# First group of attention: two of five pieces of a combination on VectorE, the last Fourier parts on three PSUM banks

## The chip, the cores and the metric

The kernel runs on one core of one Trainium2 chip. The core has five engines with an instruction queue each: TensorE (PE; its weight loads are shown as PEld), VectorE (DVE), ScalarE (ACT), GpSimd (POOL) and SyncE (SP, which issues transfers). On-chip memory is SBUF; the results of TensorE land in PSUM, which has eight banks of 128 partitions by 512 f32 columns. The metric is the device time of one execution in microseconds, as the median of several runs; less is better.

## What is computed

One layer of a diffusion backbone for 256 context ("prompt") tokens and 2048 latent tokens of width 1024: a modulated norm, one projection to queries, keys, values and Fourier channels, differential attention in four heads, a Fourier transform over positions and channels in four groups of 128 channels, an output projection, and a squared-ReLU MLP. What matters here, cut from the reference:

```python
def one_block(qblk):                      # differential attention
    s = jnp.einsum('bqhmd,bkhmd->bhmqk', qblk, k).astype(jnp.float32) * scale
    p = jax.nn.softmax(s, axis=-1)
    a = p[:, :, 0] - lam * p[:, :, 1]
    return jnp.einsum('bhqk,bkhe->bqhe', a.astype(v.dtype), v)
...
def fourier_mix(f, w_four):
    b, n, _, _ = f.shape
    spec = jnp.fft.fft2(f.astype(jnp.float32), axes=(1, 3), norm='ortho').real.astype(f.dtype)
    return jnp.einsum('bngc,gce->bnge', spec, w_four).reshape(b, n, FOUR_WIDTH)
...
def merge(attn, four, subln_g, lam_init, w_out):
    ...
    return jnp.concatenate([a.reshape(b, n, ATTN_WIDTH), four], axis=-1) @ w_out
```

Per query and head there are two score rows (m = 0 and 1), each with its own softmax over 2560 keys; the second, scaled by lambda and the ratio of the two sums, is subtracted from the first, and the difference multiplies the values.

## The kernel before

The kernel runs through stages: norm and projection, the Fourier transform, attention, output projection and MLP. Matrix products that need f32 accuracy are made of three matmuls on split operands (`mm3`, lines 86 to 88: high by high, high by low, low by high), so an operand that comes out of PSUM is split into a rounded high part (a ScalarE cast) and a low part (a VectorE subtraction).

**The Fourier part (lines 645 to 835).** The transform over 2048 positions is folded into shorter ones. For each part and each of the four channel groups g, `ab` makes two products A and B over positions, each in a PSUM tile of the tag "ab" (five banks), and `evac` (lines 669 to 674) splits them: the cast to `abh` at L672, the subtraction into `abl` at L673. Then `yT` (lines 650 to 661) multiplies A and B by the channel matrices of the group into a tile `py` of the tag "y" (three banks), and a ScalarE copy at L661 puts it into the group's output tile `ys`, with a stride that interleaves the frequencies. All parts but the last make two such halves for a group, one for the rising and one for the mirrored frequencies. The loop over the parts (lines 819 to 833) runs "p" (the prompt), "e", "f" and "l", with 256, 256, 128 and 256 columns for A and B each; the product `py` of a group stands one group behind its A and B in program order, so that the split is done meanwhile. When a group's part "l" is copied, ScalarE issues the transfer of `ys` to DRAM (`four`, L698). The last product of part "l" of group 3 is the last TensorE work before attention.

**Attention (lines 838 to 1156).** A `Head` holds keys and values of one head, a `Group` 256 queries of it in two halves j of 128 rows. For a group, `fill(j, m, b)` writes the scores of 512 keys into one PSUM bank (two matmuls, L918), so there are 2 x 2 x 5 = 20 fills per group; `rowmax` (VectorE, L923) takes the maximum of the bank, `comb` (L926) that of the five, negated; `exp` (ScalarE, L942) writes the exponentials into `P0s` for m = 0 or `P1s` for m = 1 with their sum and thereby frees the bank. `combine(j)` (lines 944 to 966) makes the factor (L946 to L948) and adds the scaled `P1s` into `P0s`: on GpSimd in two parts of 1024 and 1536 columns, each a scaling (L964) and an addition (L965), or, as far as `vcomb` says, on VectorE in pieces of 512 columns with one instruction each (L954). Before, `vcomb` is 5 for the first group (first head, g = 0) and for the last one, and 0 for all others; it applies to j = 1 only. Then come transpositions (`tr`, L974), splitting (`ah`, L980; `al`, L985) and the product with the values (`mul`, L998).

Attention's PSUM is one pool: five banks of the tag "S", two of the tag "pt" for the transpositions and one, "po", for the output. Fills use "S". For the first and second group and for the last one, `bank` counts fills (`edge`) and lets two of seven consecutive fills use "pt" as well, because no transpositions run then.

The order of the work on every engine is that of the program text here: the events of all groups are put into a list with planned times (a step takes T, five exps), sorted, and written out under `manual_schedule`. Every engine works through its own queue in this order. The framework puts a semaphore wait where an instruction needs another engine's result or a buffer that is still in use; a PSUM tile is one bank and is handed on when its last reader is done.

Of the kernel before, what the change touches and what calls it, by code (L numbers as in the profile page):

```python
# [18 lines left out]
P = 128  # L19
# [21 lines left out]
def body(tc, a, out):  # L41
    nc = tc.nc
    ctx = ExitStack()
    with ctx:
# [599 lines left out]
        with ExitStack() as c2:  # L644
# [3 lines left out]
            pp = c2.enter_context(tc.tile_pool(name="f_p", bufs=2, space=PSUM, reuse_waits="tile"))  # L648
# [19 lines left out]

            def evac(pa, q, w, nm):
                hi = ft.tile([P, 512], F32R, tag=f"abh{q}", name=f"abh{nm}", bufs=4 - 2 * q)  # L670
                lo = ft.tile([P, 512], F32R, tag=f"abl{q}", name=f"abl{nm}", bufs=4 - 2 * q)
                nc.scalar.copy(hi[:, :w], pa[:, :w])  # L672
                V.tensor_sub(lo[:, :w], pa[:, :w], f32(hi[:, :w]))  # L673
                return hi, lo
# [8 lines left out]

            def put_prompt(g, A, B):
                y = ft.tile([P, NP], F32, tag="yp", name=f"yp{g}")
                yT(y, g, A, B, 256)
                nc.scalar.dma_start(four[g * P:g * P + P, 0:NP], y)
# [63 lines left out]
            with tc.manual_schedule():  # L751
# [3 lines left out]
                mats = {nm: [ft.tile([P] + list(a[nm].shape[1:]), F32R, tag=f"{nm}_{t}", name=f"{nm}_{t}", bufs=1)  # L755
                             for t in range(a[nm].shape[0] // P)] for nm in ("c1024", "s1024", "c512", "s512", "c256", "s256")}
# [62 lines left out]
                for n, (ea, ma, eb, mb), w, p in (  # L819
                        ("p", (lambda: PR, "c256", lambda: PR, "s256"), 256, put_prompt),  # L820
                        ("e", (lambda: EO[512, "e"], "c1024", lambda: EO[512, "o"], "s1024"), 256, put(1024)),
                        ("f", (lambda: EO[256, "e"], "c512", lambda: EO[256, "o"], "s512"), 128, put(512)),
                        ("l", (lambda: S3, "c256", lambda: S3, "s256"), 256, put(256))):
                    for g in range(4):
                        nA = ab(g, 0, ea(), MT[ma], w, n)
                        nB = ab(g, 1, eb(), MT[mb], w, n)
                        last_put(*pend)
                        last_put, pend = p, (g, nA, nB)
                        if n == "p" and g == 0:
                            k_store(0, NK[0] // P - 1, parts[0])  # L830
                        if n == "e" and g == 0:
                            q_store(LAST, parts[1])
                        prep(1)
                last_put(*pend)
# [6 lines left out]
        with ExitStack() as c3_:  # L841
# [7 lines left out]
            pS = c3_.enter_context(tc.tile_pool(name="a_ps", bufs=1, space=PSUM, reuse_waits="tile"))  # L849
# [31 lines left out]
            class Group:  # L881
                def __init__(self, hd, g):
# [8 lines left out]
                    self.vcomb = 5 if self.last else 5 if hd.h == hd.s == g == 0 else 0  # L891
# [8 lines left out]
                def bank(self, nm, tag):  # L900

                    if self.edge is not None:
                        self.edge += 1
                        tag = "pt" if self.edge % 7 > 4 else "S"
                    if self.g == 1 and self.edge == 29:
                        self.edge = None
                    return pS.tile([P, 512], F32, tag=tag, name=nm, bufs=5 if tag == "S" else 2)
# [20 lines left out]
                def exp(self, j, m, b):  # L928
# [8 lines left out]
                    else:  # L937
                        x = int(c0 >= PCUT)
                        if (j, x) not in self.p1:
# [48 lines left out]
                def mul(self, kb):  # L988
                    if self.po is None:
                        self.po = pS.tile([P, 512], F32, tag="po", name=f"po{self.nm}")  # L990
# [110 lines left out]
            for h in range(H):  # L1101
# [15 lines left out]
                for g in range(hd.ng):  # L1117
                    gr = Group(hd, g)
                    add(base - 2 * T + 0.6 * u if base else -3.03 * T, gr.qload)
# [34 lines left out]
            with tc.manual_schedule():  # L1154
                for _, _, fn, args in sorted(ev, key=lambda e: (e[0], e[1])):
                    fn(*args)
# [749 lines left out]
```

## Time and profile before

| | |
|---|---|
| runs, median (lowest to highest) | 2970.22 us (2969.95 to 2972.25) |
| the profiled execution | 2976.96 us |
| its span (first to last recorded instruction) | 2975.1 us |
| mean granted TensorE clock | 0.993 of full speed |
| first matmul of attention | 571.29 us from the span's start |
| first exponential of attention | 575.36 us |

The profile is of one execution. Engines are told apart by their busy time; each view names an instruction by its line, engine, operation, and output <- input by the program's names with buffer numbers left out, so that `Ss` is any score bank and `py` any tile of that name. "x10" counts instructions that a row takes together, and a bracket at the end of a row holds the idle time of the engine before it and the instruction that ended it. The rows that matter are shown with the prediction.

### The profile page before, as it was taken

The page shows a single profiled execution, that of the slowest core. Times are in us where ns is not written, and L with a number is a line of the kernel's source. Part 1 is how long each engine was busy: PE and PEld are TensorE (multiplying, and loading weights), DVE is VectorE, ACT ScalarE, POOL GpSimd, SP SyncE. Part 2 cuts the span into 40 slices and gives each one's busy share as a digit, 9 for nine tenths or more (in the row PEclk, how much of TensorE's full clock was granted, in tenths as well). Part 3 has the DMA queues.
Part 4 walks back from the last instruction along what each step waited for, and adds up shares of the span by engine and source line. Part 5 has one row for each costly group of instructions (what it writes and reads, how often), then busy time and mean ns, then how long its engine had stood idle before and what let it go on. Part 6 is the DMA issues. An engine that isn't in the chain of part 4 may idle for free.

```text
span 2975.1 us, 43755 instructions
## 1 busy us (share of the span) xinstructions
PE 2910.2 (98%) x15417; PEld 2518.0 (85%) x15417; DVE 2016.3 (68%) x3379; ACT 1568.3 (53%) x3540; POOL 1023.9 (34%) x839
## 2 busy tenths in 40 slices
PE   8999999989999999999999999999999999999999
PEld 4888887768888888888889999999999888888887
DVE  6666775678888888875458778777776344344554
ACT  4333322678888888864346556556555322232221
POOL 1111112169898989952222333333332000000000
PEclk9999999989999999999999999999999999999999
DMA  7777878512131211215686677676666454445563
GB/s 274 202 195 198 232 197 250 195 52 84 35 110 37 91 53 34 95 50 157 202 252 213 217 240 225 220 237 214 222 199 229 145 170 163 138 145 173 195 216 107
DMA packets 394414, 495.58 MB, mean 167 GB/s; under 512 B 26403, under 2 KB 307056, under 8 KB 391122
## 3 DMA queue, kind: packets, MB, share of 16 engines
q1 hardware_dynamic: 386560, 477.63, 50.5%
q0 software_dynamic: 2992, 7.28, 0.8%
q10 hardware_dynamic: 4642, 7.88, 0.8%
q8 instruction: 122, 2.00, 0.3%
q14 instruction: 98, 0.80, 0.1%
HBM read 315.20 MB, written 179.57 MB: 166 GB/s over the span
## 4 chain that ended last, share of the span: by engine, by line
PE 84%; ACT 8%; DVE 4%; DMA 2%; issue 1%; POOL 0%; SPq 0%; ACTq 0%; DVEq 0%; POOLq 0%
PE Ss L918 8%; PE ps L86 8%; PE ps L87 8%; PE ps L88 8%; PE pj L86 4%; PE pj L88 4%; PE pj L87 4%; PE pts L974 4%; ACT P1s L942 3%; PE po L88 2%; PE po L86 2%; PE po L87 2%; PE pA L1532 2%; PE pA L1534 2%; PE pA L1533 2%; PE pC L1534 2%
## 5 line engine op out<-in xcount | busy, mean ns | idle before, releaser
L923 DVE TENSOR_REDUCE mxs<-Ss 128x1 f32<-128x512 f32 x640 | 419.4, 687 | 86.8 <-PE Ss L918 77.9
L1227 DVE TENSOR_TENSOR sl<-sr,sh 128x768 fp32r<-128x768 f32 x168 | 161.8, 964 | 339.8 <-ACT sh L1226 339.3
L965 POOL TENSOR_TENSOR P0s<-P0s,P1s 128x1024 f32<-128x1024 f32 x124 | 365.7, 2949 | 10.4
L1226 ACT CAST sh<-sr 128x768 fp32r<-128x768 f32 x168 | 140.2, 835 | 424.9 <-PE ps L87 424.9
L942 ACT ACTIVATE P1s<-Ss,mxs 128x512 f32<-128x512 f32 x320 | 217.2, 694 | 69.3 <-DVE mxs L926 69.3
L1574 POOL TENSOR_TENSOR gs<-g,g 128x384 f32<-128x384 f32 x48 | 70.3, 1464 | 483.7 <-ACT g L1544 376.7
L86 PE MATMUL pj<-wh,hh 128*128 128x512 f32 x576 | 229.8, 399 | 0.7 <-ACT fo L374 0.7
L87 PE MATMUL ps<-tlT,sh 128*128 128x512 f32 x585 | 229.3, 392 | 0.0
L86 PE MATMUL ps<-thT,sh 128*128 128x512 f32 x585 | 229.2, 392 | 0.0
L87 PE MATMUL pj<-wl,hh 128*128 128x512 f32 x576 | 227.7, 395 | 0.7 <-DVE wl L496 0.7
L88 PE MATMUL ps<-thT,sl 128*128 128x512 f32 x585 | 227.7, 389 | 0.0
L88 PE MATMUL pj<-wh,hl 128*128 128x512 f32 x576 | 226.7, 394 | 0.0
L942 ACT ACTIVATE P0s<-Ss,mxs 128x512 f32<-128x512 f32 x320 | 215.8, 696 | 7.8 <-DVE mxs L926 7.7
L918 PE MATMUL Ss<-KS1s,Qs 128*128 128x512 f32 x640 | 199.9, 426 | 13.6 <-ACT P0s L942 11.1
L918 PE MATMUL Ss<-KS0s,Qs 128*128 128x512 f32 x640 | 198.7, 423 | 10.5 <-ACT P1s L942 9.4
L974 PEld LDWEIGHTS pts<-ident,P0s 128*128 128x128 f32 x1280 | 158.0, 141 | 51.7 <-ACT ahs L980 5.7
L974 PE MATMUL pts<-ident,P0s 128*128 128x128 f32 x1280 | 193.0, 274 | 6.3 <-DVE alp L1071 4.1
L1543 ACT ACTIVATE g<-uz 128x384 f32<-128x384 f32 x144 | 75.9, 527 | 207.1 <-DVE uz L1566 180.6
L964 POOL TENSOR_SCALAR P1s<-P1s,tots 128x1024 f32<-128x1024 f32 x124 | 166.7, 1344 | 5.6
L985 DVE TENSOR_TENSOR als<-pts,ahs 128x512 fp32r<-128x512 f32 x256 | 163.9, 681 | 5.3 <-ACT ahs L980 5.3
L86 PE MATMUL ps<-ophT,sh 128*128 128x512 f32 x423 | 165.9, 392 | 1.1 <-DVE uz L1566 1.1
L88 PE MATMUL ps<-ophT,sl 128*128 128x512 f32 x423 | 165.7, 392 | 0.0
(613 smaller groups left out, 8216.1 us busy)
## 6 DMA issues: line engine op xcount, KB each, us to landing
sr<-sd SPq DMA_DIRECT2D x84, 768.0 KB, 4.4
a<-in_w SPq DMA_DIRECT2D x184, 256.0 KB, 3.8
sd<-gs SPq DMA_DIRECT2D x192, 192.0 KB, 1.9
sd<-g SPq DMA_DIRECT2D x144, 192.0 KB, 4.1
wm<-in_w_mod SPq DMA_DIRECT2D x32, 512.0 KB, 5.3
Qs<-qd SPq DMA_DIRECT2D x32, 512.0 KB, 3.7
b<-in_w SPq DMA_DIRECT2D x64, 256.0 KB, 5.2
b<-tsum SPq DMA_DIRECT2D x64, 256.0 KB, 4.6
```

What stands on the lines that cost most here:

```text
L86: nc.tensor.matmul(ps, lh, rh, start=first, stop=False)
L87: nc.tensor.matmul(ps, lh, rl, start=False, stop=False)
L88: nc.tensor.matmul(ps, ll, rh, start=False, stop=last)
L918: nc.tensor.matmul(S[:, :w], self.Q[:, x, m, j * P:j * P + P], self.hd.KS[m][:, b * 512:b * 512 + w], start=(x == 0), stop=(x == 1))
L923: nc.vector.tensor_reduce(self.mx[j][:, m, b:b + 1], self.S[j, m, b], axis=AX.X, op=ALU.max)
L942: nc.scalar.activation(dst, S, AF.Exp, bias=self.mx[j][:, m, 6:7], accum_out=self.sm[j][:, m, b:b + 1])
L964: nc.gpsimd.tensor_scalar(p, p, tot[:, 3:4], 0.0, op0=ALU.mult, op1=ALU.add)
L965: nc.gpsimd.tensor_add(d, d, p)
L974: nc.tensor.transpose(pt[:, c:c + P], self.p0[j][:, (kb + t) * P:(kb + t + 1) * P], ident)
L985: nc.vector.tensor_sub(t, self.pt[kb], f32(self.A[kb][0]))
L1226: nc.scalar.copy(hi, src)
L1227: nc.vector.tensor_sub(lo, src, f32(hi))
```

## The change

- **The combination.** `vcomb` of the first group is 2 in place of 5: for j = 1, VectorE makes the first two pieces of 512 columns (L954), and GpSimd the remaining 1536 columns in one scaling and one addition (L964, L965).
- **The Fourier parts "f" and "l".** After part "e" the PSUM pool is closed, and a new one, `f_p2`, of three banks is opened: two of the tag "ab", one tile `py2`. `ab2` writes A and B of a group side by side into one bank and splits both with one cast and one subtraction of double width. `put2` multiplies by the channel matrices into one half (256 columns) of `py2` or the other: in part "f" (and for the last group of "e", whose product stands one group behind) both halves for a group, in part "l" the half g % 2. Each half is copied by ScalarE to `ys` as before.
- **Attention's pool** becomes three pools, "po", "pt" and "S", opened in this order, so that the banks of "S" are others than the three of `f_p2`. The first group's first ten fills use "S" alone; "pt" joins from the eleventh fill on.
- **SBUF.** Some tiles of the Fourier part (`yp`, `abE`, `abo`) are made ahead of time (`MADE`), which sets where they lie; one `P1s` tile of the first group takes a buffer of the tag "Q".
- **The order.** Events of the first group with j = 0 (`fill`, `rowmax`, `exp`, `comb`) are written under `high_priority`.

```diff
@@ -645,7 +646,8 @@
             yp = c2.enter_context(tc.tile_pool(name="f_y", bufs=1, side="right", reuse_waits="tile"))
             ft = c2.enter_context(tc.tile_pool(name="f_t", bufs=2, reuse_waits="tile"))
             fw = c2.enter_context(tc.tile_pool(name="f_w", bufs=1, reuse_waits="tile"))
-            pp = c2.enter_context(tc.tile_pool(name="f_p", bufs=2, space=PSUM, reuse_waits="tile"))
+            c2p = ExitStack()
+            pp = c2p.enter_context(tc.tile_pool(name="f_p", bufs=2, space=PSUM, reuse_waits="tile"))
             ys = [yp.tile([P, NS], F32, tag=f"ys{g}", name=f"ys{g}") for g in range(4)]
             cw = []
 
@@ -666,9 +668,10 @@
             def ab_mm(pa, g, src, mat, w, first, last):
                 mm3(pa[:, :w], src[0][:, g * P:g * P + P], src[1][:, g * P:g * P + P], mat[0], mat[1], first, last)
 
+            MADE = {}
+
             def evac(pa, q, w, nm):
-                hi = ft.tile([P, 512], F32R, tag=f"abh{q}", name=f"abh{nm}", bufs=4 - 2 * q)
-                lo = ft.tile([P, 512], F32R, tag=f"abl{q}", name=f"abl{nm}", bufs=4 - 2 * q)
+                hi, lo = MADE.pop(nm, None) or [ft.tile([P, 512], F32R, tag=f"ab{x}{q}", name=f"ab{x}{nm}", bufs=4 - 2 * q) for x in "hl"]
                 nc.scalar.copy(hi[:, :w], pa[:, :w])
                 V.tensor_sub(lo[:, :w], pa[:, :w], f32(hi[:, :w]))
                 return hi, lo
@@ -681,8 +684,33 @@
                     ab_mm(pa, g, src[t], mats[t], w, t == 0, t == n - 1)
                 return evac(pa, q, w, f"{nm}{g}_{q}")
 
+
+            def ab2(pq, g, sa, ma, sb, mb, w, nm):
+                pa = pq.tile([P, 512], F32, tag="ab", name=f"pab{nm}{g}", bufs=2)
+                for x, src, mat in ((0, sa, ma), (w, sb, mb)):
+                    for t in range(len(src)):
+                        mm3(pa[:, x:x + w], src[t][0][:, g * P:g * P + P], src[t][1][:, g * P:g * P + P], mat[t][0], mat[t][1],
+                            t == 0, t == len(src) - 1)
+                hi, lo = evac(pa, 0, 2 * w, f"{nm}{g}")
+                return (hi[:, 0:w], lo[:, 0:w]), (hi[:, w:2 * w], lo[:, w:2 * w])
+
+            def put2(n, py):
+                def go(g, A, B):
+                    k = n // 4
+                    y = ys[g].rearrange("p (j t) -> p j t", t=NS // n * 2 if n > 256 else NS // n)
+                    r, l = cw[g]
+                    w = k if n > 256 else n
+                    for x, d, si in ((0, y[:, 0:k, NS // n], 2), (1, y[:, 2 * k - 1:k - 1:-1, NS // n], 1)) if n > 256 else ((g % 2, y[:, :, 0], 2),):
+                        ps = py[:, x * 256:x * 256 + w]
+                        mm3(ps, r[:, 0, :], l[:, 0, :], A[0], A[1], True, False)
+                        mm3(ps, r[:, si, :], l[:, si, :], B[0], B[1], False, True)
+                        nc.scalar.copy(d, ps)
+                    if n == 256:
+                        nc.scalar.dma_start(four[g * P:g * P + P, NP:NT], ys[g])
+                return go
+
             def put_prompt(g, A, B):
-                y = ft.tile([P, NP], F32, tag="yp", name=f"yp{g}")
+                y = MADE.pop(f"yp{g}", None) or ft.tile([P, NP], F32, tag="yp", name=f"yp{g}")
                 yT(y, g, A, B, 256)
                 nc.scalar.dma_start(four[g * P:g * P + P, 0:NP], y)
 
@@ -752,8 +780,18 @@
 
                 ptq = [pp.tile([P, 512], F32, tag="y", name=f"pt{LAST}_{m}", bufs=3) for m in range(2)]
                 d1024 = [ft32(ft, "d", f"d1024_{t}", 4) for t in range(4)]
-                mats = {nm: [ft.tile([P] + list(a[nm].shape[1:]), F32R, tag=f"{nm}_{t}", name=f"{nm}_{t}", bufs=1)
-                             for t in range(a[nm].shape[0] // P)] for nm in ("c1024", "s1024", "c512", "s512", "c256", "s256")}
+                def mat_tiles(*nms):
+                    return {nm: [ft.tile([P] + list(a[nm].shape[1:]), F32R, tag=f"{nm}_{t}", name=f"{nm}_{t}", bufs=1)
+                                 for t in range(a[nm].shape[0] // P)] for nm in nms}
+
+                mats = mat_tiles("c1024", "s1024", "c512", "s512")
+                for g in range(2):
+                    MADE[f"yp{g}"] = ft.tile([P, NP], F32, tag="yp", name=f"yp{g}")
+                for g in range(4):
+                    MADE[f"E{g}"] = [ft.tile([P, 512], F32R, tag=f"ab{x}0", name=f"ab{x}E{g}", bufs=4) for x in "hl"]
+                for g in range(2):
+                    MADE[f"o{g}_1"] = [ft.tile([P, 512], F32R, tag=f"ab{x}1", name=f"ab{x}o{g}", bufs=2) for x in "hl"]
+                mats.update(mat_tiles("c256", "s256"))
 
                 jm, k0, kn = (fw.tile([P, P], F32, tag=x, name=x) for x in ("jm", "k0", "kn"))
                 for t in (jm, k0, kn):
@@ -816,11 +854,9 @@
                     if g:
                         prep(2)
                 last_put = put(2048)
-                for n, (ea, ma, eb, mb), w, p in (
-                        ("p", (lambda: PR, "c256", lambda: PR, "s256"), 256, put_prompt),
-                        ("e", (lambda: EO[512, "e"], "c1024", lambda: EO[512, "o"], "s1024"), 256, put(1024)),
-                        ("f", (lambda: EO[256, "e"], "c512", lambda: EO[256, "o"], "s512"), 128, put(512)),
-                        ("l", (lambda: S3, "c256", lambda: S3, "s256"), 256, put(256))):
+
+                def parts_of(n, ea, ma, eb, mb, w, p):
+                    nonlocal last_put, pend
                     for g in range(4):
                         nA = ab(g, 0, ea(), MT[ma], w, n)
                         nB = ab(g, 1, eb(), MT[mb], w, n)
@@ -831,6 +867,21 @@
                         if n == "e" and g == 0:
                             q_store(LAST, parts[1])
                         prep(1)
+
+                parts_of("p", lambda: PR, "c256", lambda: PR, "s256", 256, put_prompt)
+                parts_of("e", lambda: EO[512, "e"], "c1024", lambda: EO[512, "o"], "s1024", 256, put(1024))
+                c2p.close()
+                pq = c2.enter_context(tc.tile_pool(name="f_p2", bufs=1, space=PSUM, reuse_waits="tile"))
+                py = pq.tile([P, 512], F32, tag="y", name="py2")
+                last_put = put2(1024, py)
+                pend = pend[0], *([x[:, :256] for x in y] for y in pend[1:])
+                F_ = ("f", lambda: EO[256, "e"], "c512", lambda: EO[256, "o"], "s512", 128, put2(512, py))
+                L_ = ("l", lambda: S3, "c256", lambda: S3, "s256", 256, put2(256, py))
+                for n, ea, ma, eb, mb, w, p in (F_, L_):
+                    for g in range(4):
+                        nA = ab2(pq, g, ea(), MT[ma], eb(), MT[mb], w, n)
+                        last_put(*pend)
+                        last_put, pend = p, (g, *nA)
                 last_put(*pend)
             c2.close()
             right.close()
@@ -846,7 +897,8 @@
             at = c3_.enter_context(tc.tile_pool(name="a_t", bufs=2, reuse_waits="tile"))
             ap = c3_.enter_context(tc.tile_pool(name="a_p", bufs=5, reuse_waits="tile"))
             kp = c3_.enter_context(tc.tile_pool(name="a_kp", bufs=1, reuse_waits="tile"))
-            pS = c3_.enter_context(tc.tile_pool(name="a_ps", bufs=1, space=PSUM, reuse_waits="tile"))
+
+            pS = {x: c3_.enter_context(tc.tile_pool(name=f"a_{x}", bufs=1, space=PSUM, reuse_waits="tile")) for x in ("po", "pt", "S")}
             PCUT = 1024
 
             class Head:
@@ -888,7 +940,7 @@
                     self.edge = 20 * g - 1 if hd.h == hd.s == 0 and g < 2 else None
                     self.last = hd.h == H - 1 and g == NS // 256 - 1
 
-                    self.vcomb = 5 if self.last else 5 if hd.h == hd.s == g == 0 else 0
+                    self.vcomb = 5 if self.last else 2 if hd.h == hd.s == g == 0 else 0
 
                 def qload(self):
                     self.Q = at.tile([P, 2, 2, 256], F32R, tag="Q", name=f"Q{self.nm}", bufs=3)
@@ -901,10 +953,10 @@
 
                     if self.edge is not None:
                         self.edge += 1
-                        tag = "pt" if self.edge % 7 > 4 else "S"
+                        tag = "pt" if (self.edge if self.last else self.edge - 10) % 7 > 4 and (self.last or self.edge > 9) else "S"
                     if self.g == 1 and self.edge == 29:
                         self.edge = None
-                    return pS.tile([P, 512], F32, tag=tag, name=nm, bufs=5 if tag == "S" else 2)
+                    return pS[tag].tile([P, 512], F32, tag=tag, name=nm, bufs=5 if tag == "S" else 2)
 
                 def fill(self, j, m, b):
                     if m == 0 and b == 0:
@@ -936,6 +988,8 @@
                         dst = self.p0[j][:, c0:c0 + w]
                     else:
                         x = int(c0 >= PCUT)
+                        if (j, x) not in self.p1 and x == j == self.g == self.hd.h == self.hd.s == 0:
+                            self.p1[j, x] = f32(at.tile([P, 2, 2, 256], F32R, tag="Q", name=f"P1{nm}_{x}", bufs=3)).rearrange("p a b c -> p (a b c)")
                         if (j, x) not in self.p1:
                             self.p1[j, x] = at.tile([P, min(nk, (PCUT, 2560 - PCUT)[x])], F32, tag=f"P1{x}_{self.hd.s}", name=f"P1{nm}_{x}")
                         dst = self.p1[j, x][:, c0 - x * PCUT:c0 - x * PCUT + w]
@@ -987,7 +1041,7 @@
 
                 def mul(self, kb):
                     if self.po is None:
-                        self.po = pS.tile([P, 512], F32, tag="po", name=f"po{self.nm}")
+                        self.po = pS["po"].tile([P, 512], F32, tag="po", name=f"po{self.nm}")
                     A = self.A.pop(kb)
                     for t in range(2):
                         c = slice(t * 256, t * 256 + 256)
@@ -1116,6 +1170,8 @@
                     add(r + t * u, fn, *args)
                 for g in range(hd.ng):
                     gr = Group(hd, g)
+                    if not base:
+                        gr0 = gr
                     add(base - 2 * T + 0.6 * u if base else -3.03 * T, gr.qload)
                     for st in range(4):
                         j, m = divmod(st, 2)
@@ -1152,8 +1208,11 @@
             add(base - 16 * T, load_wout)
             
             with tc.manual_schedule():
+
+                first = [gr0.fill, gr0.rowmax, gr0.exp, gr0.comb]
                 for _, _, fn, args in sorted(ev, key=lambda e: (e[0], e[1])):
-                    fn(*args)
+                    with tc.high_priority() if fn in first and args[0] == 0 else contextlib.nullcontext():
+                        fn(*args)
 
 
         ORDER = (1, 6, 2, 7, 5, 4, 3)
```

1 line of the change is left out of this document (added).

## The prediction

> **What bounds the kernel now.** I read the page first, then the stretch from the last Fourier part into attention: the windows view, the timeline, the chain of waits in order of time.
>
> ```profile
> span 2975.1 us, 43755 instructions
> PE 2910.2 (98%) x15417; PEld 2518.0 (85%) x15417; DVE 2016.3 (68%) x3379; ACT 1568.3 (53%) x3540; POOL 1023.9 (34%) x839
> PE 84%; ACT 8%; DVE 4%; DMA 2%; issue 1%; POOL 0%; SPq 0%; ACTq 0%; DVEq 0%; POOLq 0%
> ```
>
> TensorE sets the time: 98% busy and 84% of the chain that ended last. The change leaves the count and the order of its matmuls alone, so it can only win or lose where TensorE waits or runs at a lower clock. The windows view (window, length, then busy of PE, PEld, DVE, ACT, POOL, PE clock, DMA share, GB/s) shows where that is:
>
> ```profile
> 545.00:570.00 25.00, 25.00 (x207) 24.00 (x205) 10.37 (x26) 16.25 (x41) 0.00 (x0) 1.00 0.44 179
> 575.00:580.00 5.00, 3.81 (x10) 2.01 (x10) 4.24 (x9) 4.16 (x13) 0.00 (x0) 0.80 1.02 341
> 595.00:600.00 5.00, 0.43 (x2) 0.00 (x0) 4.97 (x10) 0.10 (x1) 0.00 (x0) 0.85 0.00 0
> 600.00:605.00 5.00, 3.29 (x6) 1.62 (x6) 2.51 (x5) 3.35 (x10) 0.00 (x0) 0.50 0.00 0
> 615.00:620.00 5.00, 5.00 (x24) 4.10 (x23) 2.95 (x5) 3.22 (x10) 0.53 (x1) 0.66 0.05 20
> ```
>
> The end of the Fourier part (545 to 570 us) has no TensorE gap at all: 25.00 of 25.00. Attention's entry has them, and the clock falls to half behind the largest. The timeline (start, length, engine, line, what; in brackets the wait and its releaser) names them:
>
> ```profile
> 570.62 0.62 ACT L661 COPY ys<-py 128x256 f32<-128x256 f32 x1 [0.40 <-PE py L88]
> 571.29 2.59 PE L918 MATMUL Ss<-KS0s,Qs 128*128 128x512 f32 x10 [1.02 <-ACT ys L661]
> 572.05 3.08 DVE L923 TENSOR_REDUCE mxs<-Ss 128x1 f32<-128x512 f32 x5 [2.36 <-PE Ss L918]
> 573.72 1.10 PE L918 MATMUL Ss<-KS1s,Qs 128*128 128x512 f32 x4
> 575.36 0.69 ACT L942 ACTIVATE P0s<-Ss,mxs 128x512 f32<-128x512 f32 x1 [4.12 <-DVE mxs L926]
> 576.04 0.68 ACT L942 ACTIVATE P0s<-Ss,mxs 128x512 f32<-128x512 f32 x1
> 576.19 2.15 PE L918 MATMUL Ss<-KS1s,Qs 128*128 128x512 f32 x6 [1.37 <-ACT P0s L942]
> 579.30 0.69 ACT L942 ACTIVATE P1s<-Ss,mxs 128x512 f32<-128x512 f32 x1 [0.48 <-DVE mxs L926]
> ...
> 591.77 4.82 DVE L954 SCALAR_TENSOR_TENSOR P0s<-P1s,tots,P0s 128x512 f32<-128x512 f32 x5
> 596.52 3.07 DVE L923 TENSOR_REDUCE mxs<-Ss 128x1 f32<-128x512 f32 x5
> 599.90 0.69 ACT L942 ACTIVATE P1s<-Ss,mxs 128x512 f32<-128x512 f32 x1 [5.25 <-DVE mxs L926]
> 600.73 1.22 PE L918 MATMUL Ss<-KS0s,Qs 128*128 128x512 f32 x2 [5.29 <-ACT P1s L942]
> ```
>
> Three waits: 1.02 us of the first fill on the last Fourier copy, 1.37 us of the eighth fill (two matmuls each) on the first exp (all seven score banks are full), and 5.29 us, where five rowmax stand behind the five pieces of the combination on VectorE.
>
> **The change part by part.**
>
> (a) Three pieces leave VectorE. The spread of that line (min/median/max ns):
>
> ```profile
> L954 DVE SCALAR_TENSOR_TENSOR P0s<-P1s,tots,P0s x10: 739/747/2167, 591.8 to 1307.5; 128x512 f32<-128x512 f32 x10
> 588.27 1.55 POOL L964 TENSOR_SCALAR P1s<-P1s,tots 128x1536 f32<-128x1536 f32 x1
> 589.90 3.48 POOL L965 TENSOR_TENSOR P0s<-P0s,P1s 128x1536 f32<-128x1536 f32 x1
> 606.11 0.34 POOL L948 TENSOR_SCALAR tots<-tots,nlam 128x1 f32<-128x1 f32 x1 [12.04 <-DVE tots L947]
> ```
>
> The first piece takes 2.17 us; it ends as GpSimd's addition does (589.90 + 3.48 = 593.38, plus one ordinary piece). The other four share 4.82 - 2.17 = 2.65, so 0.66 each. The three removed are the cheap ones: 3 x 0.66 = **-2.0 us** on the 5.29-us wait (bounds: 0 if something else ends it, -2.9 by the mean, 3 x 0.96). The first piece stays slow. GpSimd gets 1.55 + 3.48 = 5.0 us inside 12.04 us of idleness; the transposes that read the last pieces come some 10 us later, so nothing on the path. Without that cover the price would be those 5.0 us.
>
> (b) The last two Fourier parts on three banks. One evacuation of double width replaces two: 8 casts and 8 subtractions fewer, beside a TensorE that doesn't wait for them, so nothing. But both halves of a transform's product (`py2`) now share one bank, and in the built program the first matmul into one half waits for ScalarE's copy of the other. Before, three banks rotated. What that costs is read from pairs of halves: the second half's first matmul (L86) and the copy of the first (ACT).
>
> ```profile
> 552.19 1.12 ACT L661 COPY ys<-py 128x256 f32<-128x256 f32 x2
> 552.69 0.33 PE L86 MATMUL py<-abhe,cwh 128*128 128x256 f32 x1
> 553.56 0.28 PE L86 MATMUL py<-abhe,cwh 128*128 128x256 f32 x1
> 553.76 1.35 ACT L661 COPY ys<-py 128x256 f32<-128x256 f32 x2 [0.19 <-PE py L88]
> ...
> 562.18 0.27 PE L88 MATMUL py<-abhf,cwl 128*128 128x128 f32 x1
> 562.29 0.28 PE L86 MATMUL py<-abhf,cwh 128*128 128x128 f32 x1
> 562.49 0.42 ACT L661 COPY ys<-py 128x128 f32<-128x128 f32 x1 [0.24 <-PE py L88]
> ...
> 569.24 0.28 PE L88 MATMUL py<-abhl,cwl 128*128 128x256 f32 x1
> 569.36 0.28 PE L86 MATMUL py<-abhl,cwh 128*128 128x256 f32 x1
> 569.56 0.67 ACT L661 COPY ys<-py 128x256 f32<-128x256 f32 x1 [0.34 <-PE py L88]
> ```
>
> Part f: the copy would end at 562.49 + 0.42 = 562.91, with about 0.06 to the matmul (the gap from 570.62 + 0.62 to 571.29 above) at 562.97 instead of 562.29: 0.68 us, for each of four groups, 2.7. Part l: 569.56 + 0.67 + 0.06 - 569.36 = 0.93, once (groups 2 and 3 stand back to back; between the others twelve matmuls cover the copy). The last group of part e, put into the new bank: the first half waits for the older bank's copy, 552.19 + 1.12 + 0.06 - 552.69 = 0.68; the second, 553.76 + 0.67 + 0.06 - 553.56 = 0.93; the following f group, whose six matmuls (0.67 us) do not cover a copy that needs 0.31 (562.49 - 562.18) + 0.67 + 0.06 from the last matmul's start, 0.3. Sum 2.7 + 0.93 + 0.68 + 0.93 + 0.3 = **+5.5 us**. Bounds: 4.1 (f and l and half of e) to 6.2 (a cast ahead of each copy on ScalarE).
>
> The Trainium skill, "PSUM — Partial Sum Buffer", section "PSUM bank collisions raise a hardware error", says that engines must be kept apart by bank and partition quadrant, not by address. Were addresses enough, these 5.5 us would be 0; no run here shows which waits could be spared.
>
> (c) Attention's score banks are other ones than the last product's, so the first fill no longer waits for the last copy: **-1.0 us** (the bracket; at most the copy's own wait and length behind the last matmul, 0.40 + 0.62 + 0.05 = 1.07; at the least 0, if the fill then waits for its weights). The marks of high priority move nothing: on all five engines the built order differs by the edits alone.
>
> (d) The first ten fills use five banks instead of seven. Before, fills 6 and 7 (the four matmuls at 573.72) were written ahead of the first exp, and the second exp series began 579.30 - 575.36 = 3.94 us behind the first. Now fill 6 waits for the first exp: 576.19 - 575.36 = 0.83 to its start, 572.05 - 571.29 = 0.76 to its rowmax; four more fills follow as exps release banks, every 0.68 (576.04 - 575.36); the last rowmax takes 0.69, and 599.90 - 596.52 - 3.07 = 0.31 pass to the exp. 0.83 + 0.76 + 4 x 0.68 + 0.69 + 0.31 = 5.3, **+1.3 us**. The next series meets the same five banks: I take another **+1.1**, a little less, as the two transposition banks join at the eleventh fill. Bounds for both together: 0 (another wait had the room) to 2.6. Later the rotation stands one bank off, and fills that waited as the one at 576.19 did can find a bank: I take **-0.7**, half of that 1.37, as an estimate between 0 and -1.4. Should the two not join as I think, a third series is late by 1.3.
>
> (e) The clock. In the chain of waits in order of time, the same work at the half and at the full clock:
>
> ```profile
> 606.60 1.22 PE Ss L918 x2
> 608.67 1.71 PE Ss L918 x4
> 610.38 0.85 PE pts L974 x4
> ...
> 628.09 0.93 PE Ss L918 x4
> 629.01 0.44 PE pts L974 x4
> 632.30 0.73 PE Ss L918 x2
> ```
>
> 0.49, 0.78 and 0.41 us more for each. The stretch at half clock runs, by the windows, from before 600 us to about 612 and again between 615 and 620; with some eight such pieces on the chain at a mean of 0.5, about 4 us are lost to it in before (an estimate). The 5.29-us gap shrinks to about 3.3 and could spare some of this. Against it: the stalls of (b). Ten matmuls of 512 columns took 2.59, at most 0.26 each; 128 columns are then worth 0.065 us but take 0.11 in part f (562.18 to 562.29), so at most 59% of the array's rate is used, and the clock stayed at 1.00. With 0.68 us added to a group's eighteen matmuls (2.0 us) it is 44%. Between 575 and 580 us ten matmuls were worth 2.6 of 5 us, 52%, and the clock fell, though most of that lack lay ahead of 576.19, in one piece. 44% in small pieces is thus near the edge and on no sure side of it. I take **+1.3 us**, between -4 (all spared) and +4 (another such stretch).
>
> The Trainium skill, "TensorE: Matmul & The Clock Gate", Part 1, puts the drop behind an idle window of about 3.4 us. By that, stalls under 1 us cost nothing in clock; the 0.80 in the window 575 to 580 us, behind a wait of 1.37, speaks against it. Where it holds, a gap of 3.3 us would just keep the clock up, which is the second rival below.
>
> Sum: -2.0 + 5.5 - 1.0 + 2.4 - 0.7 + 1.3 = **+5.5 us**. From there on attention is bound by TensorE and nothing takes the delay up. The profiled run took 2976.96 us (span 2975.1): it becomes 2982.5. The runs' median is 2970.22, 6.7 below; the same step gives **2975.7**.
>
> **The rivals.** 1 (slower, chance 0.34): the f-part stalls bring the array under the point where the clock falls, so the l part and the entry run partly at half clock. Price: the +4 of (e) instead of 1.3 gives 2978.4; it decides as soon as the point where the clock falls lies above the 44% that I work out. For it: 52% and a fallen clock from 575 to 580 us. Against it: no stall of 0.7 us alone is seen to have done it.
>
> 2 (not slower, 0.12): the smaller gap keeps the clock up, -4 in place of +1.3: +0.2, 2970.4. For it: 2 of 5.29 us go. Against: 3.3 us are left, and 595 to 600 us had 0.43 us of TensorE in five.
>
> 3 (faster, 0.10): the copies hide, as the windows' 16.25 of 25.00 on ScalarE leave room and the wait could be shorter than the profile's ends suggest: (b) 0 and (e) -4: -2.0 - 1.0 + 2.4 - 0.7 - 4 = -5.3; without the lost banks -7.7: 2962.5 to 2964.9. Against: TensorE had no slack at all there.
>
> 4 (the change does not do what it says, 0.04): VectorE's relief is void, because the first piece, 2.17 us long under GpSimd's addition, lengthens with two and the rowmax are then late for another reason: +2 on my sum, 2977.7.
>
> **How the numbers follow.** The forecast has 0.40. Measured differences under 0.2% (5.9 us) can't be told from none. The forecast at +5.5 with its own spread of 2 stands just inside: 0.24 of its 0.40 below +5.9, 0.16 above. Rival 1 is slower (0.26) or stays inside (0.08), rival 2 is the same, rival 3 faster in most of its cases (0.09), rival 4 splits evenly. Together faster 0.09, same 0.47, slower 0.44. The range, 2967 to 2982, holds all but rival 3 and the dear end of rival 1.
>
> **What would show it.** In the profile after: gaps of TensorE of 0.6 to 0.9 us, released by the copies into `ys`, in part f and the last group; the first fill without a wait but some 4.5 us later; the second exp series about 5.3 us behind the first; two pieces on VectorE and the large wait near 3.3 us; the granted clock of the f and l parts for rival 1. I am wrong if the last part shows no gaps, or if the delay at the third group of attention differs from that at the end.

## The result and the profile after

| | before | changed |
|---|---|---|
| median of 7 runs each | 2974.12 us | 2986.64 us |
| lowest to highest | 2969.95 to 2975.06 us | 2977.82 to 2988.55 us |
| profiled execution | 2976.96 us | 2986.64 us |
| its span | 2975.1 us | 2984.4 us |
| mean granted clock of its execution | 0.993 | 0.992 |

The ratio is 1.0040, with a 95% interval of 1.0027 to 1.0053: the change makes the kernel 12.5 us slower. The forecast was 2975.7 us, 5.5 us more than before, in a range that ended at 2982. Between the two profiled executions lie 9.7 us.

The windows view of the changed kernel (window, length, busy of PE, PEld, DVE, ACT, POOL, PE clock, DMA share, GB/s), over the last Fourier parts and the wait that VectorE's pieces set:

```profile
550.00:555.00 5.00, 4.29 (x34) 3.94 (x34) 2.72 (x6) 3.18 (x8) 0.00 (x0) 1.00 0.87 338
555.00:560.00 5.00, 3.95 (x32) 3.53 (x31) 0.85 (x2) 2.34 (x6) 0.00 (x0) 1.00 0.68 291
560.00:565.00 5.00, 4.52 (x23) 4.33 (x21) 0.43 (x1) 1.16 (x3) 0.00 (x0) 0.50 0.01 3
565.00:570.00 5.00, 4.52 (x22) 4.33 (x21) 0.69 (x1) 1.38 (x3) 0.00 (x0) 0.50 0.00 0
570.00:575.00 5.00, 5.00 (x30) 5.00 (x30) 0.51 (x1) 1.41 (x3) 0.00 (x0) 0.64 0.00 0
...
605.00:610.00 5.00, 1.79 (x6) 0.59 (x4) 4.97 (x9) 1.83 (x7) 4.73 (x4) 1.00 0.00 0
610.00:615.00 5.00, 3.60 (x8) 2.08 (x8) 3.14 (x6) 3.24 (x10) 1.50 (x1) 0.66 0.00 2
```

Before, 545 to 570 us stood at 25.00 of 25.00 and a clock of 1.00. Now TensorE has gaps from 550 us on, and from 560 to beyond 570 it runs at half the clock. Its timeline shows the gaps and the matmuls on both sides of the clock's fall:

```profile
556.09 0.27 PE L89 MATMUL py<-abhf,cwl 128*128 128x128 f32 x1
556.40 0.39 ACT L707 COPY ys<-py 128x128 f32<-128x128 f32 x1 [0.61 <-PE py L89]
556.85 0.33 PE L87 MATMUL py<-abhf,cwh 128*128 128x128 f32 x1 [0.48 <-ACT ys L707]
557.01 0.28 PE L88 MATMUL py<-ablf,cwh 128*128 128x128 f32 x1
557.12 0.27 PE L89 MATMUL py<-abhf,cwl 128*128 128x128 f32 x1
...
560.60 0.41 PE L87 MATMUL pabf<-c,e_0h 128*128 128x128 f32 x1
560.81 0.41 PE L88 MATMUL pabf<-c,e_0h 128*128 128x128 f32 x1
...
580.27 2.49 PE L970 MATMUL Ss<-KS0s,Qs 128*128 128x512 f32 x10
584.25 0.69 ACT L996 ACTIVATE P0s<-Ss,mxs 128x512 f32<-128x512 f32 x1 [3.08 <-DVE mxs L978]
585.08 3.41 PE L970 MATMUL Ss<-KS1s,Qs 128*128 128x512 f32 x10 [2.31 <-ACT P0s L996]
589.45 0.69 ACT L996 ACTIVATE P1s<-Ss,mxs 128x512 f32<-128x512 f32 x1 [1.75 <-DVE mxs L978]
...
603.73 2.83 DVE L1008 SCALAR_TENSOR_TENSOR P0s<-P1s,tots,P0s 128x512 f32<-128x512 f32 x2
606.48 3.07 DVE L975 TENSOR_REDUCE mxs<-Ss 128x1 f32<-128x512 f32 x5
609.78 0.69 ACT L996 ACTIVATE P1s<-Ss,mxs 128x512 f32<-128x512 f32 x1 [3.17 <-DVE mxs L978]
610.61 3.60 PE L970 MATMUL Ss<-KS0s,Qs 128*128 128x512 f32 x8 [3.22 <-ACT P1s L996]
```

Between the two halves of a group the first matmul of the second half starts 0.76 us behind the last of the first (556.09 to 556.85) where the pitch is 0.11: a stall of 0.65 us, released by ScalarE's copy. At 560 us the pitch of the same kind of matmul goes from 0.11 to 0.21 (560.60 to 560.81). The first fill has no wait any more, but comes at 580.27 instead of 571.29. The large wait behind VectorE's pieces is 3.22 us, down from 5.29.

Where the time went, by marks that both programs have; the last two columns are the distance from the start of part f, against before. "Again" is another profiled execution of the same changed kernel (e5 below). A series is five exps. The count starts at part f because the way up to it varies: the kernel before and e3, e6 and e7, whose programs are the same up to there, reach it between 550.1 and 552.9 us.

| start of | before | changed | again | changed, more | again, more |
|---|---|---|---|---|---|
| part f | 552.01 | 551.25 | 551.74 | 0 | 0 |
| part l | 560.25 | 565.18 | 563.54 | +5.7 | +3.6 |
| first fill | 571.29 | 580.27 | 575.02 | +9.7 | +4.0 |
| second series | 579.30 | 589.45 | 584.86 | +10.9 | +5.8 |
| third series | 583.50 | 595.45 | 591.28 | +12.7 | +8.1 |
| fifth series | 591.19 | 603.15 | 598.99 | +12.7 | +8.1 |
| sixth series | 599.90 | 609.78 | 605.62 | +10.6 | +6.0 |
| ninth series | 620.64 | 627.55 | 623.71 | +7.7 | +3.3 |
| last (128th) series | 1297.48 | 1304.74 | 1300.88 | +8.0 | +3.7 |
| end of span | 2975.1 | 2984.4 | 2979.5 | +10.0 | +4.6 |

Most of the loss is made in the last Fourier parts, and its size depends on whether the clock falls there. The series up to the third add 3.0 us to it, and from the fifth to the ninth 5.0 are given back.

### The profile page after: what moved, and what is told of

Same layout as the page of the kernel before. It is cut to its first block, busy times and chain, and to the rows that moved or that the text cites. A ratio compares the mean times of both kernels' runs of the same rounds, so it can differ in the third digit from the quotient of the medians.

```text
span 2984.4 us, 43736 instructions
## 1 busy us (share of the span) xinstructions
PE 2915.0 (98%) x15417; PEld 2522.3 (85%) x15417; DVE 2014.0 (67%) x3368; ACT 1567.2 (53%) x3532; POOL 1029.8 (35%) x841
## 4 chain that ended last, share of the span: by engine, by line
PE 84%; ACT 8%; DVE 4%; DMA 2%; issue 1%; POOL 0%; SPq 0%; ACTq 0%; DVEq 0%; POOLq 0%
PE Ss L970 8%; PE ps L87 8%; PE ps L88 8%; PE ps L89 8%; PE pj L89 4%; PE pj L88 4%; PE pj L87 4%; PE pts L1028 4%; ACT P1s L996 3%; PE po L89 2%; PE po L87 2%; PE po L88 2%; PE pC L1593 2%; PE pA L1591 2%; PE pB L1593 2%; PE pB L1591 2%
## 5 line engine op out<-in xcount | busy, mean ns | idle before, releaser
L1019 POOL TENSOR_TENSOR P0s<-P0s,P1s 128x1536 f32<-128x1536 f32 (+1 forms) x125 | 369.0, 2952 | 10.4
L1018 POOL TENSOR_SCALAR P1s<-P1s,tots 128x1536 f32<-128x1536 f32 (+1 forms) x125 | 168.5, 1348 | 5.7
```

What stands on the lines that cost most here:

```text
L1018: nc.gpsimd.tensor_scalar(p, p, tot[:, 3:4], 0.0, op0=ALU.mult, op1=ALU.add)
L1019: nc.gpsimd.tensor_add(d, d, p)
```

## Experiments

Eight experiments were made, e1 to e4 on one chip and e5 to e8 on another, each beside the kernel before (2974.55 us in 33 runs, 2974.45 us in 26). In most of them theory A, that the shared bank stalls TensorE and the stalls bring its use so low that the clock falls, stands against rivals that put the loss elsewhere.

**e1: the two halves in two banks.**

```diff
-                py = pq.tile([P, 512], F32, tag="y", name="py2")
+                py = [pq.tile([P, 512], F32, tag=f"y{x}", name=f"py2{x}") for x in range(2)]
...
-                        ps = py[:, x * 256:x * 256 + w]
+                        ps = py[x][:, 0:w]
```

> Edit: the changed kernel with the two halves of the last products in two banks (four banks for parts f and l), all else as changed. Theory A (the shared bank makes TensorE wait for each copy, and the lowered use lets the clock fall): the five waits on copies of 0.65 us in part f and 0.93 us in part l go, about 4.6 us less; the clock stays at 1.0 from 550 to 575 us, so about 5 us more; first fill at 571.5 to 573 us instead of 580.27; time 2975 to 2979 us, about 8 us under the changed kernel where that had its clock fall. Rival B (the two banks for A and B, instead of five, hold TensorE up, or the wider evacuation does): nothing of this, first fill still near 580 us. Rival C (the tail does not matter, the loss lies in attention's entry): first fill early, but the delay is back by the third group.

2977.5 us (2975.99 to 2980.67, 11 runs), ratio 1.0012 (1.0003 to 1.0020). Its windows:

```profile
555.00:560.00 5.00, 5.00 (x48) 5.00 (x46) 1.16 (x3) 3.05 (x9) 0.00 (x0) 1.00 0.62 265
560.00:565.00 5.00, 5.00 (x46) 5.00 (x45) 0.81 (x2) 2.38 (x6) 0.00 (x0) 1.00 0.00 0
565.00:570.00 5.00, 5.00 (x42) 4.67 (x40) 1.75 (x3) 3.20 (x6) 0.00 (x0) 1.00 0.61 251
```

TensorE is full again from 555 us to the entry and the clock stays up there, with only two banks for A and B and with the wider evacuation. The first fill comes at 571.07. That takes rival B away, and rival C too: 7 to 9 us of the time are gone with the stalls (2977.5 against 2984.9 in e5 and 2986.6). One wait of 1.2 us at the change of the pools comes in, ahead of part f's first matmul; the changed kernel has no such wait.

**e2: the stalls stay, the array is kept busy.**

```diff
                         nc.scalar.copy(d, ps)
+                        if n == 512 and x == 0:
+                            for i in range(5):
+                                nc.tensor.matmul(dm[:, 0:256], r[:, 0, :], MT["c1024"][0][0], start=True, stop=True)
...
```

`dm` is a tile in a bank of its own.

> Edit: the changed kernel with five idle matmuls of 256 columns into a spare bank between the two halves of each group of part f (work that nothing reads), which fit into the 0.65-us wait. Theory A: the waits stay, but the use of the array in part f is back to about 55%, so the clock stays at 1.0; first fill at about 575 us (571.29 less 0.8 for the earlier start, plus 4.4), 5 us under the changed kernel's 580.27; time 2979 to 2981 in nearly every run, no more spread between runs of 2978 and 2988. Rival D (the clock falls for another reason than low use, or the clock is not what costs): clock 0.5 between 560 and 573 us as before, first fill at 580 us or later.

2980.16 us (2978.75 to 2983.81, 11 runs), ratio 1.0018 (1.0010 to 1.0027). Its windows:

```profile
555.00:560.00 5.00, 5.00 (x44) 4.85 (x43) 0.60 (x2) 2.01 (x5) 0.00 (x0) 1.00 0.49 208
560.00:565.00 5.00, 5.00 (x44) 4.84 (x42) 1.07 (x2) 2.21 (x5) 0.00 (x0) 1.00 0.00 0
565.00:570.00 5.00, 5.00 (x44) 5.00 (x45) 0.76 (x3) 2.28 (x4) 0.00 (x0) 1.00 0.13 52
```

The clock stays at 1.00 in the tail. The first fill comes at 573.64; counted from the start of part f (550.17 here) it is 4.2 us late against before, not 9.7. Twenty matmuls that compute nothing make the changed kernel faster (2984.9 in e5 and 2986.6 above), because what they take was stall anyway. This is the run that parts the two halves of the loss at the first fill: 4.2 us are the stalls less the first fill's wait, the other 5.5 us the half clock. The runs lie within 5.1 us, where the changed kernel's lay within 10.7.

**e3: VectorE's relief alone**, the kernel before with `vcomb` 2 in place of 5 for the first group.

> Edit: the kernel before with two pieces on VectorE instead of five, and nothing else of the change. Theory A: the 5.29-us wait becomes 3.3; 0 to 3 us faster than before, the spread by the clock behind the wait. Rival (VectorE's relief is void, the rowmax wait on something else): no change of the 5.29-us wait.

2972.28 us (2970.88 to 2975.43, 11 runs), ratio 0.9993 (0.9984 to 1.0001). The timeline of it:

```profile
589.45 2.82 DVE L954 SCALAR_TENSOR_TENSOR P0s<-P1s,tots,P0s 128x512 f32<-128x512 f32 x2
592.19 3.07 DVE L923 TENSOR_REDUCE mxs<-Ss 128x1 f32<-128x512 f32 x5
596.40 0.74 PE L918 MATMUL Ss<-KS0s,Qs 128*128 128x512 f32 x2 [3.30 <-ACT P1s L942]
```

The two pieces take 2.82 us and the wait is 3.30, 2.0 less. The median is 2.3 us lower, but the interval still holds no difference at all. Part (a) of the change does in the trace what it was taken to do.

**e4: seven banks for the first ten fills.** With the old rule the later fills of the first two groups also take their banks in the old rotation; the rest is as changed.

```diff
-                        tag = "pt" if (self.edge if self.last else self.edge - 10) % 7 > 4 and (self.last or self.edge > 9) else "S"
+                        tag = "pt" if self.edge % 7 > 4 else "S"
```

> Edit: the changed kernel with the old rule for the first ten fills (seven banks, two of those of the transpositions among them), all else as changed. Theory A: the second exp series begins 3.9 us behind the first instead of 5.2, the later ones likewise; 2 to 3 us less than the changed kernel at the end of the first group, at equal clock in the tail. Rival (the banks' count at the entry is covered by other waits): same distance of the series, same time.

2981.42 us (2977.53 to 2988.08, 11 runs), ratio 1.0023 (1.0014 to 1.0032). In its profile the clock fell in the tail as in the changed kernel's, from 557.2 to 574.3 us. The fills:

```profile
580.88 2.49 PE L970 MATMUL Ss<-KS0s,Qs 128*128 128x512 f32 x10
583.21 1.09 PE L970 MATMUL Ss<-KS1s,Qs 128*128 128x512 f32 x4
584.85 0.69 ACT L996 ACTIVATE P0s<-Ss,mxs 128x512 f32<-128x512 f32 x1 [3.08 <-DVE mxs L978]
585.68 2.07 PE L970 MATMUL Ss<-KS1s,Qs 128*128 128x512 f32 x6 [1.38 <-ACT P0s L996]
```

Fills 6 and 7 run ahead of the first exp again, the second series follows at 588.71, 3.86 us behind the first, and the fifth series starts 19.4 us behind the first fill, against 22.9 in the changed kernel. But the ninth starts 46.7 behind it, against 47.3: of 3.5 us 0.6 are left. So the five banks cost what they should where they act. What is given back goes between the seventh and the ninth series, and from the sixth to the ninth e4's profile has 13.7 us at half clock, the changed kernel's 6.8. The medians of e4 and the changed kernel are not told apart (2981.42, and 2984.93 in e5, with ranges that overlap).

**e5: the changed kernel once more.**

> The changed kernel once more, unaltered, for the spread of its runs and beside other kernels on one chip. Theory A (the clock in the last Fourier parts falls in some executions and not in others, as the stalls bring the use near the edge): two groups of runs, near 2978 to 2980 us with a mean clock of 0.994 or 0.995 and near 2985 to 2989 us with 0.991 or 0.992; and if the profile is of the fast group, the clock is 1.0 from 555 to 575 us and the first fill near 575 us. Rival (a fixed extra delay in the tail): one group, at 2983 to 2988 us.

2984.93 us (2979.82 to 2988.53, 5 runs), ratio 1.0033 (1.0021 to 1.0046). The five times are 2979.82, 2981.63, 2984.93, 2984.99 and 2988.53 us, with mean clocks of 0.994, 0.993, 0.993, 0.992 and 0.991: a slope, not the two groups that were expected. The profile is of the second of them:

```profile
555.00:560.00 5.00, 4.02 (x33) 3.59 (x31) 0.85 (x2) 2.52 (x6) 0.00 (x0) 1.00 0.78 332
560.00:565.00 5.00, 4.45 (x37) 4.31 (x38) 0.42 (x1) 1.59 (x5) 0.00 (x0) 1.00 0.01 3
565.00:570.00 5.00, 4.52 (x40) 4.38 (x39) 1.38 (x2) 2.64 (x5) 0.00 (x0) 1.00 0.00 0
```

The same program with the same gaps (4.02 and 4.45 of 5), and here the clock did not fall in the tail. The first fill comes at 575.02, 4.0 us late counted from part f. So the stalls, less the first fill's wait, cost 4.0 us where the clock stays up (4.2 in e2), and the fall of the clock, where it comes, about 5.7 us more (9.7 - 4.0).

**e6: no piece on VectorE**, the kernel before with `vcomb` 0 for the first group.

> Edit: the kernel before with no piece of the first group's second combination on VectorE; GpSimd makes all five (1024 and 1536 columns). Theory A (VectorE's pieces ahead of the five rowmax set the large wait, GpSimd has time): the first piece too, 2.17 us long beside GpSimd's addition, goes; the 5.29-us wait of before becomes about 0.5 to 1, the first exp behind it 4.5 to 4.8 us earlier than before; time 3 to 6 us under before. Rival (GpSimd then is late for the transpositions): the first transposition or the one of the second part waits for the GpSimd addition, and the gain is lost.

2969.39 us (2967.46 to 2972.5, 11 runs), ratio 0.9984 (0.9976 to 0.9993): faster than both kernels.

```profile
595.62 0.69 ACT L942 ACTIVATE P1s<-Ss,mxs 128x512 f32<-128x512 f32 x1 [0.48 <-DVE mxs L926]
595.84 2.35 POOL L965 TENSOR_TENSOR P0s<-P0s,P1s 128x1024 f32<-128x1024 f32 x1
596.45 0.73 PE L918 MATMUL Ss<-KS0s,Qs 128*128 128x512 f32 x2 [0.52 <-ACT P1s L942]
599.81 3.45 POOL L965 TENSOR_TENSOR P0s<-P0s,P1s 128x1536 f32<-128x1536 f32 x1
603.16 1.06 PE L974 MATMUL pts<-ident,P0s 128*128 128x128 f32 x4
```

The 5.29-us wait is 0.52. The sixth series starts 3.9 us behind the fifth (591.68), where before it was 8.7: 4.8 us less. GpSimd's first addition ends at 598.2, five microseconds ahead of the first transposition at 603.16, which waits for nothing; the second one ends at 603.3, and the transpositions that need it come later.

**e7: as e6, with the array kept busy at the entry.** Ahead of ten fills that wait, and of the very first, 43 matmuls of 512 columns go into the output bank, which holds nothing yet.

```diff
-                    self.vcomb = 5 if self.last else 5 if hd.h == hd.s == g == 0 else 0
+                    self.vcomb = 5 if self.last else 0
...
+                    if self.hd.h == self.hd.s == 0:
+                        if self.g == 0 and self.po is None:
+                            Group.spare = self.po = pS.tile([P, 512], F32, tag="po", name=f"po{self.nm}")
+                        for i in range({0: 3, 7: 5, 12: 2, 14: 2, 17: 2, 22: 2, 27: 2, 32: 3, 33: 6, 35: 7, 40: 9}.get(20 * self.g + 10 * j + 5 * m + b, 0)):
+                            nc.tensor.matmul(Group.spare, self.Q[:, 0, m, j * P:j * P + P], self.hd.KS[m][:, 0:512], start=True, stop=True)
```

> Edit: as the run before, plus 43 idle matmuls of 512 columns into the output bank, which is still unused, ahead of those fills of the first three groups that wait for a bank; nothing reads them, the first product clears the bank. Theory A (the entry loses about 4 us to the half clock, and the clock follows the use of the array, not single gaps): clock 1.0 from 570 to 625 us, 3 to 4 us less than the run before, less spread between runs; time 2964 to 2968. Rival (the clock at the entry costs nothing, or does not follow the use): same time as the run before.

2968.19 us (2965.48 to 2969.13, 10 runs), ratio 0.9979 (0.9970 to 0.9988), the fastest of all. Its windows, and below them those of e6:

```profile
595.00:600.00 5.00, 4.84 (x21) 3.13 (x20) 2.32 (x6) 3.26 (x11) 4.92 (x3) 1.00 0.00 0
600.00:605.00 5.00, 5.00 (x27) 3.88 (x26) 4.60 (x8) 3.95 (x11) 4.74 (x5) 1.00 0.23 86
605.00:610.00 5.00, 5.00 (x34) 4.19 (x33) 4.15 (x9) 4.63 (x13) 4.92 (x3) 1.00 0.05 20
```

```profile
595.00:600.00 5.00, 3.20 (x10) 1.40 (x8) 2.83 (x6) 3.59 (x12) 4.83 (x4) 0.87 0.00 0
600.00:605.00 5.00, 3.21 (x10) 2.37 (x10) 2.00 (x6) 3.69 (x11) 4.82 (x4) 0.50 0.00 0
```

The clock stays at 1.00 (in e6 it is 0.50 from 600 to 605 us), and the ninth series starts 9.6 us earlier than before counted from part f, against 7.8 in e6. (The profile is of e7's fastest execution, 2965.48 us.) The median gains 1.2 us on e6, less than the 3 to 4 that were expected. One reason may be that without VectorE's pieces the stretch at half clock was already down to 6.8 us in e6's profile.

**e8: two banks for the halves and seven for the first fills**, the edits of e1 and e4 together.

> Edit: the changed kernel with the last products' halves in two banks and with seven banks for the first ten fills: what is left of the change are VectorE's two pieces, the wider evacuation and the free score banks. Theory A: no stall in part f, second exp series 3.9 us behind the first; at the end of the first group up to 2 us under the run with two banks alone, less what the clock takes back; time 2973 to 2977, no better than the kernel before with two pieces alone (2972), as the group of part e that comes into the new bank still waits for its copies. Rival (five banks cost nothing at the end): the same as with two banks alone, 2977.5.

2975.78 us (2971.53 to 2978.44, 11 runs), ratio 1.0008 (0.9999 to 1.0017). It is not told apart from before, 1.7 us under e1 and 3.5 above e3, which has only VectorE's part of it. The change without its stalls gains nothing that can be measured in the time; in the traces its useful parts are (a), 2.0 us of a wait, and the first fill's wait that goes. e8's profile has the 1.2-us wait ahead of part f again, as e1's has; what else keeps e8 above e3 stays open.

## Why the prediction was wrong

By its steps:

- **(a) three pieces off VectorE, -2.0:** right. From the fifth to the sixth series 6.63 us instead of 8.71, 2.1 less; alone in e3, 2.0 less. Looked at from the pieces that stay, the step missed the better edit: the one that costs most, 2.17 us beside GpSimd's addition, is the first, and e6 shows that GpSimd has time for all five.
- **(b) and (c), +5.5 and -1.0 at the first fill:** right in mechanism, 0.3 to 0.5 off in size. 4.5 was forecast; 4.0 (e5) and 4.2 (e2) are measured where the clock stays up. A half in part f stalls for 0.65 us, 0.68 was taken; the first fill's wait is gone. The term that is most off is the first half of part e's last group: 0.68 was taken, as if it waited for both copies of the 552.19 row, but in the changed kernel its first matmul starts 0.34 us behind the last matmul of part f's first A and B (551.77 to 552.11), and before it was 0.16 (552.53 to 552.69).
- **(d) +1.3 and +1.1 for five banks:** 5.20 us between the first two series instead of 3.94, +1.3 as forecast; +1.8 at the next, where +1.1 was taken because the transposition banks were to join at the eleventh fill. By the diff's rule the count only starts there, and the first fill in one of them is the sixteenth. The -0.7 for the later rotation isn't seen. From the sixth to the ninth series the changed kernel does need less, 17.8 us where before needs 20.7, but that goes with the clock: with the old rotation the stretch takes 20.7 us where 13.7 of it are at half clock (e3, e4) and 18.2 where 9.9 are (e8); with the new one it takes 18.0 with 9.7 (e1). So the rotation is worth about 0.2 us, and the other 2.8 or so belong to (e). e7, all of it at full clock, needs 16.1.
- **The marks of high priority move nothing:** nothing in the trace speaks against it; it wasn't run without them.
- **(e) the clock, +1.3 within -4 to +4:** this is the step that failed. The mechanism was named, in (e) and as the first rival, with a use of 44% as the point in doubt; its price in the tail was wrong. I read the price from the entry's half-clock stretch, where about 4 us are lost between waits, and took a third of it. In the tail nothing waits but TensorE: at half clock each matmul's pitch goes from 0.11 to 0.21, so 13.6 us at half clock (560.0 to 573.6 in the changed kernel's profile) cost up to half of that, 6.8 us; 5.7 are measured. In e4's profile the fall lasted 17.1 us, and the first fill is 11.1 us late counted from part f, 7.1 beyond the 4.0. The bound of +4 was no bound for that stretch, and the range ended at 2982 because of it. In e2, whose profile has no fall in the tail, the median is 5.6 us above before, close to the forecast's +5.5.
- **What else was off, and cancels:** with 5.7 in place of 1.3 the sum is 9.9, against the 9.7 us between the two profiled executions, but that it fits so well is luck. The entry gave back nearly 3 us of clock, (d) cost 0.6 more than forecast without its rotation, and between the ninth series and the end of the span another 2.3 us are lost that stand in no term.
- **Rival 1** was the case that came, at 0.34, and its 2978.4 is too low for the same reason.
- **The base:** the forecast stood on a median of three runs, 2970.22 us. Seven runs gave 2974.12 and 33 gave 2974.55, so about 4 us of the distance from the forecast to 2986.64 are the base's. Against the profiled run the forecast was 2982.5.

The changed kernel's profile has 2.0 us more at the end of attention (last series +8.0, end +10.0), of which the execution in e5 has 0.9 (+3.7, +4.6). In the changed kernel's windows the granted clock is 0.77 from 1315 to 1320 and 0.89 from 1320 to 1325 us; before, the low clock fell from 1300 to 1305. That the place of it makes the 2 us is only argued.

## What to carry to other kernels

A stall that is small for itself is priced with what it does to the clock: add up the use of the array over some microseconds, not the longest gap, and where the use falls to a third or so (it was 0.33 and 0.36 of the columns where the clock fell here), price a whole stretch at half clock in a place where TensorE never waits, not by a stretch where it waits anyway. Before work is shared out between two engines, look whether the other has time for all of it, and whether the piece that stays is the dear one. And take the base from as many runs as the forecast needs.

## What the runs showed of the hardware

The clock falls without any long gap. In the changed kernel no gap from 554 us to the fall at 560 is over 0.76 us from matmul to matmul (one of 0.98, from 552.81, lies ahead), and TensorE is 3.95 of 5 us busy from 555 to 560 us; at 560 the clock is half. The same program with 4.02 of 5 kept it (e5). The stretches at half clock last whole multiples of 3.41 us in these traces: before, one such step from 578.0, four from 598.5 and one from 615.6. Where these steps fall against the stalls differs between the two executions, which may be what decides; that was not shown.

Four matmuls of 512 columns take 1.71 us at half clock (the row at 608.67 in the prediction), so at the full rate one is worth 0.21 us. Worked out from the matmuls' columns at that rate, the last step before 560 us in the changed kernel streamed at 0.33 of that rate; in e5 the lowest step of part f had 0.38, and in e4, where the clock fell at 557.2 us, the step before had 0.36. By themselves these would fit an edge. But other steps, worked out in the same way, passed below it without a fall: 0.28 from 1334.8 us in the changed kernel's profile, 0.26 from 1296.5 us in e7, and 0.30 to 0.32 right behind a stretch at half clock in e1, e5 and e6. So low use lets the clock fall, and with the use raised it stayed up (e1, e2), but no edge comes out of these figures.

The Trainium skill, "TensorE: Matmul & The Clock Gate", Part 1, ties the drop to an idle window of about 3.4 us. These traces don't bear that out: here it comes with gaps of less than 1 us. Filling the gaps with matmuls that nobody reads held the clock at 1.00 in both places where it was tried (e2, e7).

A matmul of 128 columns has a pitch of 0.11 us at full clock, hardly less than the 0.12 of one with 256 columns (569.24 to 569.36 in the profile before), so at 128 columns something else than the columns sets it. At half clock it goes to 0.21, so that part slows with the clock too.
